# Weaving all attention projections of a mixing layer with the inverse of its blocks, on one Trainium2 core

## The chip, the cores and the metric

The kernel runs as one program on one core of a Trainium2 chip. The metric is the device time of one execution in microseconds (us). A profiled execution adds a trace of every engine: PE is TensorE's matmuls, PEld its weight loads, DVE is VectorE, ACT is ScalarE, POOL is GpSimd, SP is the engine that issues most DMAs.

## The reference

The reference is a network of two blocks on 512 positions of width 1024 in float32. The first (gated MLP, chunked attention, two feed-forward parts) is not touched. The second has a mixing layer and a mixture of 64 experts. The mixing layer is what the change is about: one input projection feeds eight heads of an attention with forget gates ("fox") and eight heads of a linear recurrence ("rwkv7"), and both are joined by an output projection.

```
h = rms_norm(x, norm1_g) * (1 + sc1) + sh1
z = h @ w_in
y_fox  = fox_mixer(z[..., :FOX_COLS], ...)     # q, k, v, g of 512 columns each, gates
y_rwkv = rwkv7_mixer(z[..., FOX_COLS:], ...)   # r, k, v of 512 columns each, low-rank gates
x = x + g1 * (concatenate([y_fox, y_rwkv]) @ w_out)

fox:   k = a_k * shift_prev(k) + (1 - a_k) * k         # v the same way, with a_v
       q = rms_norm(q, qn_g); k = rms_norm(k, kn_g)
       p = softmax(q k^T * scale + (cum_i - cum_j), causal)
       o = rms_norm(p v, on_g) * sigmoid(g)
rwkv7: Sa = S a_t
       S  = S * w_t + Sa b_t + v_t k_t                 # one 64x64 state per head, 512 steps
       y_t = S r_t
```

## The kernel before, in words

The mixing layer works on transposed data, features on the partitions and the 512 positions along the free axis. Heads go in pairs: a pair is 128 features. There are four pairs of rwkv and four of fox.

**Projections.** `zdense` (L880) makes 128 columns of a projection. `wpiece` (L888) loads the 512 KB weight piece (`zraw`, on SP's queue), ScalarE rounds it to `zhi`, and the engine in `self.zlo` subtracts to get the low part `zlo` (L899). `zmm` (L902) then adds three products for each of eight slices of the inner dimension (L907, L908, L909: high by high, high by low, low by high), 24 matmuls of 512 columns. The buffers `zraw`, `zhi` and `zlo` are double.

**The rwkv side.** The recurrence is done in four time chunks of 128. `rwkv_pair` (L950) makes the operands of one pair: the two gate products (`lw` L963, `la` L967), the projection of k, a normalization (the head sum `hs<-sq`), the scaled operands `at` and `bt`, two copies of `bt` padded with zeros on GpSimd (`BP`, L1008), the Gram products `pg` (L1013), their masked copy `g` on DVE (L1015) which goes to DRAM in `gab`, then the projections of r and v, and a closing head sum (`hs<-rk`, L869 by way of L1028). `solve` (L1034) loads the blocks of all Gram matrices as `XL` and inverts 32-row triangular blocks by forward substitution: for each of 31 columns a product (`soltmp<-XL`, L1051 or L1055) and a reduction (L1052 or L1056), all on DVE and each needing the one before; then a copy (L1057), the way out to DRAM and back. After that `rwkv_front` and `rwkv_back` work through 16 blocks (4 chunks by 4 pairs); the first instruction of a block on TensorE is the product `mg<-xx,gz` at L1104.

**The fox side.** `fox_z` (L1263) makes for pair m the four projections k, q, v, g. k and v are mixed with their shifted copies in `shift_mix`: three GpSimd operations on `d` (L1279 to L1281) and a DVE addition (L1282). `fox_qkv` (L1296) normalizes k and q (head sum on TensorE, a chain on DVE and ScalarE) and transposes v. `fox_att` (L1327) is the softmax attention of one pair: scores `pS`, transposed probabilities `pT`, products `pO`.

**What sets the order.** The program is written in one order, and a scheduler reorders each engine's instructions by a simulated timeline. `mixing` (L1472) issues the four rwkv pairs, then `fox_z(0)`, `fox_qkv(0)` and `fox_z(1)`; then the inverse; then everything else through `weave` (L1382). There each stream is a generator that yields an estimate of its TensorE time and of a pause, and the stream with the earliest due time is issued next, in the order of the letters of `WEAVE`. The streams: `rwkv_fronts` (which begins by waiting `SOLVE` = 34 us of simulated time), `rwkv_backs`, `fox_rest` (the attentions, begins after `ATT` = 28 us), `fox_qkvs`, `fox_zs`, `rwkv_outs` and `mix_begin` (the first pieces of the output projection). In the weave `self.zlo` is GpSimd, before it DVE. `tc.issue_after(x)` adds an edge to the scheduler's order on an instruction's own engine: what is issued inside stands behind x in that engine's queue; instructions of other engines are not held by it.

```
for m in range(4):
    self.rwkv_pair(m, R)
for m in range(2):
    for _ in self.fox_z(m):
        pass
    if m == 0:
        for _ in self.fox_qkv(m):
            pass
```

After the layer, the experts' buffers take over the memory of the mixing layer.

Of the kernel before, what the change touches and what calls it, by code (L numbers as in the profile page):

```python
# [11 lines left out]
AF = mybir.ActivationFunctionType  # L12
# [25 lines left out]
class Builder:  # L38
# [260 lines left out]
    def col(self, n, k):  # L299
        r, _ = self.cols[n]  # L300
        return self.colt[:, r + k:r + k + 1]
# [648 lines left out]
    def rwkv_pair(self, m, R):  # L950

        self.mark(f"rwkv_pair{m}")
        nc = self.nc
        sl = slice(m * 128, m * 128 + 128)
        col = lambda n: self.col(n, m)
        T = lambda n, b=1: R.tile([128, S], F32, name=n, tag=n, bufs=b)
        c4 = lambda t: t.rearrange("p (c t) -> p c t", c=NT)

        def out(i, t):
            nc.sync.dma_start(self.fd[m, :, :, i, :].rearrange("c f t -> f c t"), c4(t))  # L960

        ps = self.ps.tile([128, S], F32, name="lw", tag="rk", bufs=2)
        nc.tensor.matmul(ps, self.dup[:, sl], self.twd, start=True, stop=True)  # L963
        s = T("s", 2)
        nc.scalar.activation(s, ps, AF.Sigmoid, bias=col("rw_w0_2"))
        ps = self.ps.tile([128, S], F32, name="la", tag="rk", bufs=2)
        nc.tensor.matmul(ps, self.dup[:, sl], self.tad, start=True, stop=True)  # L967
        ah = T("ah", 2)
        nc.scalar.activation(ah, ps, AF.Sigmoid, bias=col("rw_a0_2"))
        cs = T("cs", 2)  # L970
        nc.vector.tensor_tensor_scan(cs, self.scan_mask, s, 0.0, op0=ALU.mult, op1=ALU.add)

        F = self.F[m]
        mid = self.z2.tile([128, NT, 1], F32, name=f"mid{m}")
        nc.vector.tensor_copy(mid, c4(cs)[:, :, 63:64])
        nc.vector.tensor_sub(F, c4(cs)[:, :, 127], mid[:, :, 0])
        nc.vector.tensor_add(F[:, 0:NT - 1], F[:, 0:NT - 1], mid[:, 1:, 0])
        nc.scalar.activation(F, F, AF.Exp, scale=-self.E05)
        nc.vector.tensor_sub(c4(cs), c4(cs), mid.to_broadcast([128, NT, 128]))
        nc.gpsimd.tensor_sub(s, cs, s)  # L980
        Em = T("Em", 2)
        nc.scalar.activation(Em, cs, AF.Exp, scale=self.E05)
        nc.scalar.activation(cs, cs, AF.Exp, scale=-self.E05)
        exp = nc.scalar.activation(s, s, AF.Exp, scale=-self.E05)
        Ep, Ex = cs, s
        if m == 0:
            with self.tc.issue_after(exp.ins):
                self.fox_forget(R)
        k = T("k")
        self.zdense(((self.RW0 + 512 + 128 * m, 128),), lambda ps: self.mixed(4 + m, ps, k))  # L990
        kk, sq = T("kk"), T("sq")
        nc.scalar.activation(kk, k, AF.Copy, scale=col("rw_k_k_2"))
        nc.scalar.activation(sq, kk, AF.Square)
        hs = self.head_sums(sq, "rk")
        xe, y, n1 = T("xe"), T("y"), T("n1")
        nc.vector.tensor_scalar(xe, hs, 1e-24, None, op0=ALU.max)
        self.newton_rsqrt(xe, y, n1, sq)
        nc.vector.tensor_mul(kk, kk, y)
        at, bt, kt, kn = T("at"), T("bt"), T("kt"), T("kn")
        nc.vector.scalar_tensor_tensor(at, kk, -1.0, Ex, op0=ALU.mult, op1=ALU.mult)  # L1000
        out(1, at)
        nc.gpsimd.tensor_mul(kk, kk, ah)
        nc.vector.tensor_mul(bt, kk, Em)
        out(2, bt)

        BP = self.BP
        for j in range(2):
            nc.gpsimd.tensor_copy(BP[j][64 * j:64 * j + 64], bt[64 * j:64 * j + 64])  # L1008
        for c in range(NT):
            cc = slice(c * 128, c * 128 + 128)  # L1010
            pg = self.ps.tile([128, 2, 128], F32, name="pg", tag="rk", bufs=2)
            for j in range(2):
                nc.tensor.matmul(pg[:, j], BP[j][:, cc], at[:, cc], start=True, stop=True)  # L1013
            g = R.tile([128, 2, 128], F32, name="g", tag="g", bufs=2)
            nc.vector.tensor_mul(g, pg, self.mS[:, None, :].to_broadcast([128, 2, 128]))  # L1015
            nc.sync.dma_start(self.gab[:, c, 2 * m:2 * m + 2, :], g)
        nc.scalar.activation(kn, ah, AF.Identity, scale=col("rw_k_a_2"), bias=self.cols2[:, 16 + m:17 + m])
        nc.vector.tensor_mul(kn, kn, k)
        nc.vector.tensor_mul(kt, kn, Em)
        out(3, kt)  # L1020
        r, rt, rk, v = T("r"), T("rt"), T("rk"), T("v")
        self.zdense(((self.RW0 + 128 * m, 128),), lambda ps: self.mixed(m, ps, r))
        nc.vector.tensor_mul(rt, r, Ep)
        out(0, rt)
        nc.vector.scalar_tensor_tensor(rk, r, col("rw_r_k_2"), kn, op0=ALU.mult, op1=ALU.mult)
        self.zdense(((self.RW0 + 1024 + 128 * m, 128),), lambda ps: self.mixed(8 + m, ps, v))
        out(4, v)
        hs = self.head_sums(rk, "rk")  # L1028
        last = nc.vector.tensor_mul(rk, hs, v)
        nc.sync.dma_start(self.svd[m], rk)  # L1030
        with self.tc.issue_after(last.ins):
            self.x1(2 * m)
# [230 lines left out]
    def fox_z(self, m):  # L1263

        self.mark(f"fox_z{m}")
        nc = self.nc
        scr = self.foxscr
        T = lambda n, b=1: self.fox.tile([128, S], F32, name=n, tag=n, bufs=b)
        mix = []
        for i in range(2):  # L1270
            t = T(f"mixb{i}")
            for j in range(2):
                nc.sync.dma_start(t[64 * j:64 * j + 64], scr[8 + 8 * i + 2 * m + j:9 + 8 * i + 2 * m + j].to_broadcast([64, S]))
            mix.append(t)

        def shift_mix(z, g, ps):
            d = T("d")
            nc.scalar.copy(z, ps)
            nc.gpsimd.tensor_sub(d[:, 1:], z[:, :S - 1], z[:, 1:])  # L1279
            nc.gpsimd.tensor_scalar(d[:, 0:1], z[:, 0:1], -1.0, None, op0=ALU.mult)  # L1280
            nc.gpsimd.tensor_mul(d, d, g)  # L1281
            nc.vector.tensor_add(z, z, d)  # L1282

        zk, zq, zv = T("zk", 2), T("zq", 2), T("zv", 2)
        sg = self.sgm[m] = T("sgm", 4)
        self.zdense(((512 + 128 * m, 128),), lambda ps: shift_mix(zk, mix[0], ps))
        yield 5.2, 0.9
        self.zdense(((128 * m, 128),), lambda ps: nc.scalar.copy(zq, ps))
        yield 5.2, 0.9
        self.zdense(((1024 + 128 * m, 128),), lambda ps: shift_mix(zv, mix[1], ps))  # L1290
        yield 5.2, 0.9
        self.zdense(((1536 + 128 * m, 128),), lambda ps: nc.scalar.activation(sg, ps, AF.Sigmoid))
        yield 5.2, 0.9
        self.zs[m] = zk, zq, zv

    def fox_qkv(self, m):  # L1296
# [110 lines left out]
    def rwkv_fronts(self, W, W2):  # L1407
        yield 0.0, self.SOLVE
        for c in range(NT):
# [11 lines left out]
    def fox_rest(self, W):  # L1421
        yield 0.0, self.ATT
        for m in range(4):
# [2 lines left out]
            self.nfox = m + 1  # L1426

    def fox_zs(self):
        for m in range(2, 4):
            yield from self.fox_z(m)  # L1430

    def fox_qkvs(self):
        for m in range(1, 4):
            yield lambda: m in self.zs and self.nfox > m - 2
            yield from self.fox_qkv(m)

# [29 lines left out]

    KORDER = (0, 1, 2, 4, 5, 3, 6, 7)
    WEAVE = "abfqzmo"
    SOLVE = 34.0
    ATT = 28.0  # L1470

    def mixing(self):  # L1472
        tc, nc, a = self.tc, self.nc, self.a
# [17 lines left out]
        with self.pool(name="rp", bufs=1) as R:  # L1491
            self.BP = [R.tile([128, S], F32, name=f"BP{j}") for j in range(2)]
            for j in range(2):
                nc.gpsimd.memset(self.BP[j][64 * (1 - j):64 * (1 - j) + 64], 0.0)
            with self.tc.issue_after(self.last_x.ins):
                self.x1_rstd(R)
            self.rwkv_lora(R)
            self.fps.close()
            self.mmtags = (("mm", 2),)
            self.zps = ExitStack()  # L1500
            self.ps = self.zps.enter_context(self.pool(name="zps", bufs=1, space=PSUM))
            for m in range(4):
                self.rwkv_pair(m, R)
            for m in range(2):
                for _ in self.fox_z(m):
                    pass
                if m == 0:
                    for _ in self.fox_qkv(m):
                        pass
        self.zps.close()  # L1510
        self.mmtags, self.zlo = (("fs", 2),), nc.gpsimd
        self.ps = self.zps.enter_context(self.pool(name="zps2", bufs=1, space=PSUM))
        with self.pool(name="ck", bufs=1) as W:
            with self.pool(name="sol", bufs=1) as sol:
# [992 lines left out]
```

## Time and profile before

| | |
|---|---|
| three runs | 2319.68, 2321.45, 2327.68 us (median 2321.45) |
| profiled execution, own time | 2325.68 us |
| its span in the trace | 2323.6 us |
| mean granted clock of TensorE, share of full | 0.978 |
| TensorE matmul busy | 2194.9 us, 94% of the span |
| VectorE busy | 1385.3 us, 60% |
| ScalarE busy | 1020.4 us, 44% |
| GpSimd busy | 425.0 us, 18% |

The span is the time from the first to the last instruction in the trace, 2.1 us less than the execution's own time. The shares are means over the whole program. The mixing layer takes the stretch from about 1160 us to 1640 us, where the page's row of TensorE in 40 slices has its two lowest inner digits (8 and 6) and the row of the granted clock its only 8 and 6. All times below are microseconds from the start of the span.

### The profile page before, as it was taken

The page shows a single profiled execution, that of the slowest core. Times are in us where ns is not written, and L with a number is a line of the kernel's source. Part 1 is how long each engine was busy: PE and PEld are TensorE (multiplying, and loading weights), DVE is VectorE, ACT ScalarE, POOL GpSimd, SP SyncE. Part 2 cuts the span into 40 slices and gives each one's busy share as a digit, 9 for nine tenths or more (in the row PEclk, how much of TensorE's full clock was granted, in tenths as well). Part 3 has the DMA queues.
Part 4 walks back from the last instruction along what each step waited for, and adds up shares of the span by engine and source line. Part 5 has one row for each costly group of instructions (what it writes and reads, how often), then busy time and mean ns, then how long its engine had stood idle before and what let it go on. Part 6 is the DMA issues. An engine that isn't in the chain of part 4 may idle for free. (4 is left out here: it accounts for less than half of the span.)

```text
span 2323.6 us, 31933 instructions
## 1 busy us (share of the span) xinstructions
PE 2194.9 (94%) x11699; PEld 1669.0 (72%) x11699; DVE 1385.3 (60%) x2479; ACT 1020.4 (44%) x1759; POOL 425.0 (18%) x354
## 2 busy tenths in 40 slices
PE   8999999999999999999889969999999999999995
PEld 6888888888777888888766657776666757554662
DVE  3658837854887686477557693775444837421343
ACT  4336525534886454345455524652423526211231
POOL 3023203310000322122302440002112111111110
PEclk9999999999999999999999986999999999999998
DMA  4335535435221434344045533226379999999895
GB/s 159 100 119 188 161 96 181 146 100 143 64 64 55 154 118 145 127 135 152 31 119 145 136 92 91 76 71 208 144 268 384 343 327 390 327 333 375 277 388 206
DMA packets 243810, 414.78 MB, mean 179 GB/s; under 512 B 35077, under 2 KB 135779, under 8 KB 243653
## 3 DMA queue, kind: packets, MB, share of 16 engines
q1 hardware_dynamic: 233444, 393.87, 48.8%
q0 software_dynamic: 5184, 13.71, 3.2%
q10 hardware_dynamic: 5024, 5.15, 0.9%
q8 instruction: 93, 1.52, 0.3%
q14 instruction: 65, 0.52, 0.1%
HBM read 378.93 MB, written 40.22 MB: 180 GB/s over the span
## 5 line engine op out<-in xcount | busy, mean ns | idle before, releaser
L93 DVE TENSOR_TENSOR wlo<-wraw,whi 128x2048 fp32r<-128x2048 f32 (+3 forms) x83 | 182.6, 2200 | 208.3 <-ACT whi L92 207.9
L135 PE MATMUL mm<-sgh,whi 128*128 128x512 f32 x768 | 300.8, 392 | 0.9 <-DVE hT L204 0.9
L136 PE MATMUL mm<-sgl,whi 128*128 128x512 f32 x768 | 299.3, 390 | 0.0
L137 PE MATMUL mm<-sgh,wlo 128*128 128x512 f32 x768 | 297.6, 389 | 0.0
L92 ACT CAST whi<-wraw 128x2048 fp32r<-128x2048 f32 (+3 forms) x83 | 146.2, 1761 | 211.2 <-PE mm L136 158.9
L746 POOL TENSOR_TENSOR adaacc<-adaacc,adaw 128x512 f32<-128x512 f32 x84 | 147.6, 1757 | 433.9 <-ACT adaw L745 430.7
L2181 POOL DMA_INDIRECT racc<-y,idx x60 | 88.8, 1479 | 470.3 <-DVE y L2171 401.3
L135 PEld LDWEIGHTS mm<-sgh,whi 128*128 128x128 f32 x768 | 144.2, 188 | 30.9 <-issue 1.5
L137 PEld LDWEIGHTS mm<-sgh,wlo 128*128 128x128 f32 x768 | 144.2, 188 | 30.4 <-issue 0.2
L136 PEld LDWEIGHTS mm<-sgl,whi 128*128 128x128 f32 x768 | 144.2, 188 | 29.8 <-issue 0.5
L2125 PE MATMUL pg<-er,xh 128*64 128x512 f32 (+1 forms) x768 | 152.2, 607 | 9.6 <-DMA er<-in_exp_w_up 9.6
L2054 ACT CAST eh<-er 128x512 fp32r<-128x512 f32 x200 | 116.3, 620 | 80.0 <-DMA er<-in_exp_w_up 42.7
L135 PE MATMUL mm<-ach,whi 128*128 128x512 f32 (+1 forms) x374 | 141.4, 378 | 0.0
L137 PE MATMUL mm<-ach,wlo 128*128 128x512 f32 (+1 forms) x374 | 140.9, 377 | 0.0
L136 PE MATMUL mm<-acl,whi 128*128 128x512 f32 (+1 forms) x374 | 140.8, 377 | 0.0
L2058 DVE TENSOR_TENSOR el<-er,eh 128x512 fp32r<-128x512 f32 x200 | 125.9, 685 | 13.6 <-ACT eh L2054 13.2
L2125 PEld LDWEIGHTS pg<-er,xh 128*64 128x64 f32 (+1 forms) x768 | 46.3, 130 | 105.8 <-issue 103.7
L907 PE MATMUL mm<-nmh,zhi 128*128 128x512 f32 (+2 forms) x264 | 106.3, 404 | 10.5 <-DVE k L877 5.8
L2136 ACT ACTIVATE sg<-pg 128x256 f32<-128x256 f32 x40 | 15.4, 384 | 214.8 <-PE pg L2125 214.5
L908 PE MATMUL mm<-nml,zhi 128*128 128x512 f32 (+2 forms) x264 | 103.7, 393 | 1.4 <-DVE nml L809 1.4
L909 PE MATMUL mm<-nmh,zlo 128*128 128x512 f32 (+2 forms) x264 | 102.9, 390 | 1.8 <-DVE zlo L899 1.8
L2171 DVE TENSOR_TENSOR y<-py,g2b 128x512 f32<-128x512 f32 x76 | 52.3, 690 | 87.6 <-PE py L2168 87.6
(702 smaller groups left out, 5187.2 us busy)
## 6 DMA issues: line engine op xcount, KB each, us to landing
er<-in_exp_w_gate SPq DMA_DIRECT2D x128, 512.0 KB
er<-in_exp_w_up SPq DMA_DIRECT2D x128, 512.0 KB
er<-in_exp_w_down SPq DMA_DIRECT2D x64, 1024.0 KB
wraw<-in_f_w_in SPq DMA_DIRECT2D x32, 1024.0 KB
adaw<-in_ada_w SPq DMA_DIRECT2D x96, 256.0 KB
wraw<-in_f_w_down SPq DMA_DIRECT2D x16, 1024.0 KB
zraw<-in_w_in SPq DMA_DIRECT2D x30, 512.0 KB
wraw<-in_a_w_in SPq DMA_DIRECT2D x8, 1024.0 KB
```

Of the source, the lines that this page charges most:

```text
L92: nc.scalar.copy(hi[:, :n], raw[:, :n])
L93: nc.vector.tensor_sub(lo[:, :n], raw[:, :n], hi[:, :n])
L135: nc.tensor.matmul(to, wh[:, cols], xh, start=first, stop=False)
L136: nc.tensor.matmul(to, wh[:, cols], xl, start=False, stop=False)
L137: nc.tensor.matmul(to, wl[:, cols], xh, start=False, stop=last)
L746: nc.gpsimd.tensor_add(acc, acc, t)
L907: nc.tensor.matmul(ps[:n, part], hi[:, k, :n], xh, start=first and k == ks[0], stop=False)
L908: nc.tensor.matmul(ps[:n, part], hi[:, k, :n], xl, start=False, stop=False)
L909: nc.tensor.matmul(ps[:n, part], lo[:, k, :n], xh, start=False, stop=last and k == ks[-1])
L2054: nc.scalar.copy(hi, r)
L2058: nc.vector.tensor_sub(lo, r, hi)
L2125: nc.tensor.matmul(job["pg"][b:b + n], x[:, c:c + n], job["raw"][j][h][:, k % 4] if whole else job["gu"][j][k][w], start=k == 0 and i == 0 ...
```

## The change

All sixteen fox projections are issued in the weave, none before the inverse. Each of them is put behind the last Gram product on TensorE by `issue_after(self.last_gram.ins)`. In the weave the low parts are made on VectorE. The weave's simulated waits are 52 instead of 34 us for the blocks and 45 instead of 28 us for the attentions.

```diff
@@ rwkv_pair
-                nc.tensor.matmul(pg[:, j], BP[j][:, cc], at[:, cc], start=True, stop=True)
+                self.last_gram = nc.tensor.matmul(pg[:, j], BP[j][:, cc], at[:, cc], start=True, stop=True)
@@ fox_z
-        self.zdense(((512 + 128 * m, 128),), lambda ps: shift_mix(zk, mix[0], ps))
-        yield 5.2, 0.9
-        self.zdense(((128 * m, 128),), lambda ps: nc.scalar.copy(zq, ps))
-        yield 5.2, 0.9
...
+        for c, evac in ((512, lambda ps: shift_mix(zk, mix[0], ps)), (0, lambda ps: nc.scalar.copy(zq, ps)),
+                        (1024, lambda ps: shift_mix(zv, mix[1], ps)),
+                        (1536, lambda ps: nc.scalar.activation(sg, ps, AF.Sigmoid))):
+
+            with self.tc.issue_after(self.last_gram.ins):
+                self.zdense(((c + 128 * m, 128),), evac)
+            yield 5.2, 0.9
@@ fox_zs, fox_qkvs
-        for m in range(2, 4):
+        for m in range(4):
             yield from self.fox_z(m)
...
-        for m in range(1, 4):
+        for m in range(4):
             yield lambda: m in self.zs and self.nfox > m - 2
@@ weave
-    SOLVE = 34.0
-    ATT = 28.0
+    SOLVE = 52.0
+    ATT = 45.0
@@ mixing
-            for m in range(2):
-                for _ in self.fox_z(m):
-                    pass
-                if m == 0:
-                    for _ in self.fox_qkv(m):
-                        pass
         self.zps.close()
-        self.mmtags, self.zlo = (("fs", 2),), nc.gpsimd
+        self.mmtags, self.zlo = (("fs", 2),), nc.vector
```

The scheduler's answer to this is seen in the order of the instructions on an engine. The first place is TensorE between the closing head sum of pair 2 (`hs<-rk`) and the Gram products of pair 3. Before, the queue begins there with:

```order
L869 MATMUL hs<-rk,blk 128x512
L907 MATMUL mm<-nmh,zhi 128x512
L908 MATMUL mm<-nml,zhi 128x512
L909 MATMUL mm<-nmh,zlo 128x512
L869 MATMUL hs<-sq,blk 128x512
L963 MATMUL lw<-twd,dup 128x512
L967 MATMUL la<-tad,dup 128x512
L907 MATMUL mm<-nmh,zhi 128x512
```

The last of these rows is the start of further projection matmuls, which go on until pair 3's Gram products. Now the same place is, on TensorE, from pair 2's closing head sum to pair 3's:

```order
L869 MATMUL hs<-rk,blk 128x512
L963 MATMUL lw<-twd,dup 128x512
L967 MATMUL la<-tad,dup 128x512
L869 MATMUL hs<-sq,blk 128x512
L1013 MATMUL pg<-at,BP_9343 128x128 x2
L1013 MATMUL pg<-at,BP_9344 128x128 x2
L1013 MATMUL pg<-at,BP_9343 128x128
L1013 MATMUL pg<-at,BP_9344 128x128
L1013 MATMUL pg<-at,BP_9343 128x128
L1013 MATMUL pg<-at,BP_9344 128x128
L869 MATMUL hs<-rk,blk 128x512
L907 MATMUL mm<-nmh,zhi 128x512
```

The projections of k, r and v of pair 3 stand ahead of pair 2's Gram products now, and no projection stands between the two pairs' Gram products. The first fox projection is the last row. Between pair 1's and pair 2's Gram products 48 projection matmuls are left of 72. Behind the last Gram product, nine projections (216 matmuls) stand ahead of the first block product; the other seven stand among the rows of the blocks.

The second place is VectorE inside the inverse (`soltmp` and `XL` are its steps, `zlo` a projection's low part, `zk<-zk,d` the addition of the shifted mix). Before:

```order
L1051 TENSOR_TENSOR soltmp<-XL 128x128
L1052 TENSOR_REDUCE XL<-soltmp 128x2x8
L1051 TENSOR_TENSOR soltmp<-XL 128x162
L1052 TENSOR_REDUCE XL<-soltmp 128x2x9
L1051 TENSOR_TENSOR soltmp<-XL 128x200
L1052 TENSOR_REDUCE XL<-soltmp 128x2x10
L1051 TENSOR_TENSOR soltmp<-XL 128x242
L1052 TENSOR_REDUCE XL<-soltmp 128x2x11
L1051 TENSOR_TENSOR soltmp<-XL 128x288
```

In this piece the steps follow each other without anything between them. Now the same steps on VectorE are:

```order
L1051 TENSOR_TENSOR soltmp<-XL 128x128
L1052 TENSOR_REDUCE XL<-soltmp 128x2x8
L1282 TENSOR_TENSOR zk<-zk,d 128x512
L1051 TENSOR_TENSOR soltmp<-XL 128x162
L1052 TENSOR_REDUCE XL<-soltmp 128x2x9
L1051 TENSOR_TENSOR soltmp<-XL 128x200
L1052 TENSOR_REDUCE XL<-soltmp 128x2x10
L1051 TENSOR_TENSOR soltmp<-XL 128x242
L899 TENSOR_TENSOR zlo<-zraw,zhi 128x1024
L1052 TENSOR_REDUCE XL<-soltmp 128x2x11
L1051 TENSOR_TENSOR soltmp<-XL 128x288
L1052 TENSOR_REDUCE XL<-soltmp 128x2x12
```

A low part and an addition of the mix stand between steps; over the whole inverse eight low parts and four such additions do.

The third place is TensorE in the second block, from its product `mg<-xx,gz` at L1134 on (`pT`, `pO` and `pS` are the attention's). Now:

```order
L1134 MATMUL mg<-xx,gz_10292 64x64 x2
L1340 MATMUL pS<-ka_9327,qa_9325 128x384
L1156 MATMUL pr<-tm,gg 128x64
L1110 MATMUL pt<-ident,ft 128x128 x3
L1357 MATMUL pO<-vn,PT 128x64
L1352 MATMUL pT<-ident,P 128x128 x2
L907 MATMUL mm<-nmh,zhi 128x512
L908 MATMUL mm<-nml,zhi 128x512
L909 MATMUL mm<-nmh,zlo 128x512
```

The last three rows are the start of the first of the seven projections that stand among the blocks; before, no fox projection is left behind the first block product. (Lines of the changed kernel behind L1292 are one lower than before.)

## Rows read from the trace of the kernel before

**Rows 1.** Busy time by stretch: us, PE, PEld, DVE, ACT, POOL, PEclk, DMA share, GB/s.

```profile
1170.40:1252.30 81.90, 71.22 (x294) 53.78 (x294) 50.28 (x72) 44.75 (x59) 8.76 (x8) 0.96 0.47 132
1252.30:1318.10 65.80, 61.96 (x272) 47.92 (x271) 46.76 (x67) 40.24 (x52) 22.50 (x18) 1.00 0.44 123
1318.10:1408.00 89.90, 65.92 (x274) 50.11 (x273) 68.10 (x102) 28.00 (x44) 41.26 (x39) 0.85 0.47 114
1408.00:1439.00 31.00, 30.11 (x195) 24.71 (x196) 10.80 (x37) 10.65 (x27) 0.00 (x0) 0.50 0.28 80
1439.00:1600.40 161.40, 152.82 (x1310) 117.73 (x1309) 115.60 (x333) 83.31 (x213) 9.51 (x25) 1.00 0.27 81
```

**Rows 2.** Timeline of TensorE at the milestones: start, us, instruction, [idle before, releaser].

```profile
1243.52 1.05 PE L1013 MATMUL pg<-at,BP 128*128 128x128 f32 x8
...
1247.15 1.13 PE L869 MATMUL hs<-rk,blk 128*128 128x512 f32 x2 [1.13 <-DVE g L1015]
...
1269.08 1.05 PE L1013 MATMUL pg<-at,BP 128*128 128x128 f32 x8
...
1322.11 1.02 PE L869 MATMUL hs<-rk,blk 128*128 128x512 f32 x2
...
1407.97 0.43 PE L1104 MATMUL mg<-xx,gz 128*32 128x32 f32 x8 [1.39 <-DMA xx<-xdr]
```

**Rows 3.** Longest wait of TensorE, 1318 to 1408 us: total, times, longest.

```profile
PE pT L1353 <- ACT P L1345: 14.8, 1, 14.8
```

**Rows 4.** Timeline of GpSimd: the padded copies of pair 2.

```profile
1264.95 2.14 POOL L1008 COPY BP<-bt 64x512 f32<-64x512 f32 x2 [0.86 <-DVE bt L1003]
```

**Rows 5.** Timeline of VectorE: a low part and an operation of 512 columns.

```profile
1199.27 1.22 DVE L899 TENSOR_TENSOR zlo<-zraw,zhi 128x1024 fp32r<-128x1024 f32 x1
...
1335.46 0.69 DVE L1309 TENSOR_SCALAR xe<-hs 128x512 f32<-128x512 f32 x1
```

**Rows 6.** Timeline from the masked copies to the first step of the inverse.

```profile
1246.67 0.88 DVE L1015 TENSOR_TENSOR g<-pg,mS 128x256 f32<-128x256 f32 x2 [0.40 <-DMA gab<-g]
...
1320.09 0.76 DVE L1015 TENSOR_TENSOR g<-pg,mS 128x256 f32<-128x256 f32 x2 [5.16 <-DMA gab<-g]
...
1326.21 5.07 SPq L1043 DMA_DIRECT2D XL<-gab  x4
...
1335.07 0.36 DVE L1051 TENSOR_TENSOR soltmp<-XL 128x2 f32<-128x2 f32 x1 [3.24 <-DMA XL<-gab]
```

**Rows 7.** VectorE busy during the inverse: its products and reductions through soltmp; everything.

```profile
1335.00:1393.00 58.00, 44.03 (x62) 0.84 0.33 93
...
1335.00:1393.00 58.00, 55.41 (x82) 0.84 0.33 93
```

**Rows 8.** Timeline inside the inverse: two operations of GpSimd, four of VectorE.

```profile
1346.79 2.39 POOL L899 TENSOR_TENSOR zlo<-zraw,zhi 128x1024 fp32r<-128x1024 f32 x1 [5.08 <-ACT zhi L898]
1351.11 1.30 POOL L1281 TENSOR_TENSOR d<-d,mixb 128x512 f32<-128x512 f32 x1
...
1346.95 2.63 DVE L1051 TENSOR_TENSOR soltmp<-XL 128x200 f32<-128x200 f32 x1
...
1350.01 0.94 DVE L1051 TENSOR_TENSOR soltmp<-XL 128x242 f32<-128x242 f32 x1
...
1351.43 1.54 DVE L1051 TENSOR_TENSOR soltmp<-XL 128x288 f32<-128x288 f32 x1
...
1389.74 2.80 DVE L1057 COPY XL<-XL 128x1024 f32<-128x1024 f32 x1
```

**Rows 9.** Timeline of TensorE: first and last of 72 projection matmuls.

```profile
1340.09 0.47 PE L907 MATMUL mm<-nmh,zhi 128*128 128x512 f32 x1
...
1356.29 0.40 PE L909 MATMUL mm<-nmh,zlo 128*128 128x512 f32 x1
```

**Rows 10.** Timeline of TensorE: a projection after an idle stretch, eleven matmuls apart.

```profile
1189.04 0.79 PE L907 MATMUL mm<-nmh,zhi 128*128 128x512 f32 x1 [5.77 <-DVE k L877]
...
1193.41 0.40 PE L908 MATMUL mm<-nml,zhi 128*128 128x512 f32 x1
```

## What the change does to the time, predicted

> **What bounds the kernel now.** I read the engine busy times by stage first [rows 1]. From the first pair of the mixing layer to the first weight piece of its output projection (1170 to 1600 us) TensorE is busy 382 of 430 us, so most of what it does there is on the path, and what can be won is the idle part and the part at half clock. The reader should see where these are: the pairs up to 1252 (10.7 us idle), the stretch between the last Gram product and the first block (24.0 us idle, granted clock 0.85) and the first 31 us of the blocks (granted clock 0.50, which is 1.2 GHz). Next comes the timeline of TensorE at the milestones: Gram products of pair 1 and 2, the head sum that closes the last pair (1322.11), the first block product (1407.97) [rows 2]. The last Gram product starts a serial chain that no matmul can shorten: its masked copy goes to DRAM, comes back as XL, DVE inverts 32-row blocks in 62 small steps, the result goes to DRAM and back. In the list of waits of TensorE for that stretch the longest is one of 14.8 us on a softmax that stands behind the inverse on DVE [rows 3]. After 1640 us come the experts; their buffers reuse the mixing layer's memory, so I pass a shift of 1600 us through to the end one to one.
>
> **The change, part by part.** I follow four milestones, in this profiled execution (span 2323.6, own time 2325.68; the median of the runs is 2321.45, so 4.2 us under it).
>
> 1. *The last Gram comes earlier.* In the new order TensorE has no projection between pair 2's Gram products and pair 3's (order pieces in the section on the change); seven of the eight moved projections, and one set of normalizations, leave the stretch before the last Gram. Until 1252 nothing differs. Then TensorE has 48 matmuls instead of 72 and is through at about 1263.7, but pair 2's Gram products need both padded copies of POOL, ready at 1264.95 + 2.14 = 1267.1 [rows 4], against 1269.08 now [rows 2]. From there pair 3 is a latency chain on DVE, ACT and POOL. Its length is seen one pair earlier, where no attention work stood in it: pair 1's Gram starts at 1243.52, pair 2's could start at 1267.1, 23.6 us. The new chain has no projection low part in it (1.22 on DVE [rows 5]) and no next pair's k (0.7, estimated from the other 512-column DVE operations [rows 5]), so 21.7: pair 3's Gram at 1288.8. Pair 1 then took 3.6 us to its closing head sum (1243.52 to 1247.15): 1292.4, against 1322.11. **-29.7 us.** Bounds: -31 if the first Gram products go as soon as the first padded copy is there; -27 if the chain keeps its 23.6 and half clock adds to the Grams. I take the middle, since the dropped operations are on DVE's queue, which the chain uses. The price is that TensorE now idles some 20 us in pair 3.
>
> 2. *Gram to inverse.* Now 13.0 us pass from the head sum to the first step of the inverse (1335.07), among them a masked copy that waits 5.16 us for the DMA of the one before, and an XL load issued at 1326.21 behind two weight pieces and two gate rows on SP's queue [rows 6]. In the new order none of these stands there; pair 1's copy waited 0.4 us [rows 6]. With 1.9 us for the last masked copy's DMA and the 8.9 us from the XL issue to the first step I get 1303.7, 11.3 us. **-1.7 us** (bounds 0 and -3).
>
> 3. *The inverse itself.* It takes 57.4 us (1335.07 to 1392.5). DVE is busy 55.4 us in the window, 44.0 of them with the steps' 62 instructions [rows 7]. Seven steps are far longer than their neighbours: 2.63 us beside POOL's low part of 2.39 us, while the next but one, larger, takes 0.94 [rows 8]. Interpolating between neighbours the seven are 9.3 us too long, and the final copy some 1.6: about 10.9 us lost to POOL. Four of POOL's low parts lie inside. With the low parts on DVE those blockings go, but eight low parts now stand between the steps in DVE's order, 1.15 us each once overlap with a dependent step is counted (1.22 alone [rows 5]): +9.2. POOL's shift-mix stays on POOL: three sets lie inside, 1.3 us each by the step that took 1.54 beside one, where 0.68 would fit [rows 8]: +3.9. Pair 0's two normalizations now lie inside whole, one did before, less softmax work: +0.8. So -10.9 + 9.2 + 3.9 + 0.8 = **+3.0 us**. Bounds: -5 if the sets of POOL cost nothing, +8 if each blocks for its whole 2.6 us and a low part waits for its cast.
>
> The Trainium skill (SBUF — State Buffer, "Who interferes with whom") says that DVE and GpSimd share a port pair as an exclusive lock: a two-input DVE operation and a GpSimd operation that reads SBUF exclude each other, and the later one waits in full. The 2.63 us step agrees with that. By its rule the three remaining sets could cost up to their whole length, and the term would be +6.6 instead of +3.0, the sum 3.6 us worse; I keep the row's price, since most sets fall partly on operations with one input.
>
> 4. *Inverse to first block.* 15.5 us of transfers (1392.5 to 1407.97), unchanged: **0**. TensorE's rows ahead of the first block product are nine projections and four softmax steps, all ready before: it waits for xx as now. First block at 1407.97 - 29.7 - 1.7 + 3.0 = 1379.6.
>
> 5. *The blocks.* Before, all sixteen projections were done at the first block. In the new order nine are; seven are spread over blocks 2 to 12. One projection is 24 matmuls; 72 of them start from 1340.09 to 1356.29 [rows 9], 0.228 apart, so 5.47 us each, **+38.3 us**. One normalization, one set of transposes and two softmax steps more are left: **+2.0**. Can the blocks hide them? From 1439 to 1600 TensorE is busy 152.8 of 161.4 us [rows 1], so there are 8.6 us of holes, partly in the tail. Half clock costs 15 us of the 31 [rows 1]. The first woven projection stands behind two blocks, which at 1.2 GHz take some 24 us; after an idle stretch a projection is back at full clock after some ten matmuls, as the two rows from 1189.04 on show (0.79 us, then 0.40) [rows 10]. So the slow stretch shrinks by a few us: I take **-3** for clock and holes together. Bounds: 0 (the fillers wait for their low parts as often as they fill), and -23.6 (all holes and all of the clock's cost).
>
> Sum: -29.7 - 1.7 + 3.0 + 38.3 + 2.0 - 3.0 = **+8.9 us**. On the median: 2330.4, so I say **2330 us**. In one sentence: the Gram comes 30 us earlier, by moving 38 us of TensorE's work from a stretch where it was nearly free, since the pair chain left holes for it, to the blocks, where TensorE has none.
>
> **The rivals.**
>
> *Faster: the clock and the holes pay for the weave.* The place is the first 30 us of blocks. If TensorE comes out of the inverse at 2.4 GHz, because dense projections stand right before the first block, the 15 us are won, and the 8.6 us of holes are filled too. Then the sum is +8.9 + 3.0 - 23.6 = -11.7, 2310 us. It decides when the granted clock of the first two blocks is 1.0. For it: nine projections fill the wait. Against it: DVE hands out their low parts over the whole inverse, so they come apart by more than their length and the last softmax steps leave TensorE idle, as the 14.8 us wait does now. Chance 0.17.
>
> *No net effect: the inverse gets shorter.* If POOL's rest costs nothing and the pair chain starts 1 us sooner, the sum is +8.9 - 8 - 1 = 0, 2321 us. For it: the 10.9 us lost now are large. Against: DVE's queue is full there. Chance 0.12.
>
> *Much slower: DVE's queue couples the inverse to TensorE.* Low parts wait for weight pieces, casts and freed buffers; DVE works in order, so each such wait delays the steps behind it. With +8 in place of +3 on the inverse, no relief in clock or holes, and 5 more in the tail, where the last attention now ends beside the last blocks: +21.9, 2343 us. Chance 0.13. That the change does not do what it says is ruled out by the order.
>
> **How the numbers follow.** The forecast has 0.58, with its own range 2322 to 2340. A measurement of this kernel tells 0.3%, 7 us, from no change, so the limits are 2314.5 and 2328.4. Forecast: 0.37 of its 0.58 lies above 2328.4, 0.21 inside. Slower rival: 0.13 slower. Faster rival: 0.14 faster, 0.03 same. No net effect: 0.03 faster, 0.08 same, 0.01 slower. Slower 0.51, same 0.32, faster 0.17. The range 2310 to 2345 leaves out about half of the faster rival and half of the slower one, some 0.17.
>
> **What would show it.** In the new profile: last Gram near 1291, with TensorE mostly idle from 1272 to 1288 and a granted clock at 0.5 there; first inverse step near 1304; 60 us to its copy; first block near 1380; the output projection's first piece, now at the end of the last window of [rows 1], 9 us later. Steps of 2.4 us or more should be gone from the inverse, and DVE should show eight low parts in it. I am wrong in step 1 if the Gram is not before 1300, in step 3 if the inverse takes under 54 or over 66 us, in step 5 if blocks 1 to 16 and the tail take under 215 us, where I expect 229.

## The result and the profile after

The changed kernel takes 2346.93 us (median of four runs, 2339.15 to 2347.98) against 2321.43 us before (median of four runs, one more than above); the ratio is 1.0099, with a 95% interval from 1.0077 to 1.0121. It is slower by one per cent. The profiled execution took 2346.36 us with a span of 2344.6 us, 21.0 us over the span before. The medians are 25.5 us apart, since the profiled execution of the kernel before was 4 us slower than its median. The page's first lines, against 2194.9, 1385.3 and 1020.4 us before:

```profile
span 2344.6 us, 31944 instructions
...
PE 2203.4 (94%) x11699; PEld 1675.2 (71%) x11699; DVE 1384.5 (59%) x2489; ACT 1015.5 (43%) x1754; POOL 399.8 (17%) x344
...
PEclk9999999999999999999998889989999999999998
```

The milestones first: TensorE's timeline, the rows that answer to [rows 2], and the two ends of the inverse on VectorE.

```profile
1266.78 1.38 PE L1013 MATMUL pg<-at,BP 128*128 128x128 f32 x8 [2.66 <-POOL BP L1008]
...
1288.92 4.08 PE L1013 MATMUL pg<-at,BP 128*128 128x128 f32 x16 [11.12 <-POOL BP L1008]
...
1293.40 1.13 PE L869 MATMUL hs<-rk,blk 128*128 128x512 f32 x2 [0.40 <-DVE g L1015]
...
1376.76 0.43 PE L1104 MATMUL mg<-xx,gz 128*32 128x32 f32 x8 [0.23 <-DMA xx<-xdr]
...
1613.93 0.50 PE L907 MATMUL mm<-ysh,zhi 128*128 128x512 f32 x1 [0.35 <-ACT zhi L898]
```

```profile
1301.62 0.86 DVE L1051 TENSOR_TENSOR soltmp<-XL 128x2 f32<-128x2 f32 x1 [5.04 <-DMA XL<-gab]
...
1360.18 1.08 DVE L1057 COPY XL<-XL 128x1024 f32<-128x1024 f32 x1
```

Pair 3's Gram products start at 1288.92. The closing head sum comes 28.7 us earlier than before, the first block 31.2 us earlier, and yet the last row, which answers to the end of the windows of [rows 1], comes 13.4 us later. (The prediction calls it the output projection's first piece. It is the third of eight: the first two stand among the blocks, and the output projection's first product starts at 1562.74 us before and at 1588.94 us now.) The same stretches as in [rows 1], cut at the new milestones (columns as there):

```profile
1170.40:1252.30 81.90, 71.22 (x295) 53.87 (x294) 49.95 (x72) 44.66 (x59) 8.76 (x8) 0.96 0.45 131
1252.30:1290.00 37.70, 22.27 (x79) 14.81 (x79) 27.34 (x44) 19.96 (x27) 8.69 (x8) 0.76 0.39 118
1290.00:1376.80 86.80, 69.26 (x282) 53.02 (x283) 68.18 (x112) 29.07 (x44) 20.09 (x29) 0.87 0.47 114
1376.80:1407.80 31.00, 28.92 (x204) 23.31 (x205) 16.60 (x41) 15.28 (x36) 0.00 (x0) 0.82 0.23 64
1407.80:1613.80 206.00, 193.73 (x1486) 151.95 (x1484) 127.58 (x352) 92.59 (x225) 18.58 (x34) 0.94 0.28 85
```

Read these rows as a balance of TensorE. Its work is the same in both kernels, so the length of the mixing layer is that work, plus the time in which TensorE idles, plus what half clock costs. I worked the last one out from windows of 2.5 us: busy time times what the granted clock lacks to 1. From 1170 us to the first transposes behind the layer (`ph<-ident,hT`):

| | length | idle | cost of half clock | work at full clock |
|---|---|---|---|---|
| before | 473.9 | 48.3 | 22.9 | 402.7 |
| changed | 491.9 | 60.8 | 28.2 | 402.9 |

Each row is one execution, and half clock differs between executions of one kernel: the mean granted clock of the kernel before went from 0.974 to 0.982 in its runs. The 18.0 us are 12.5 of idle time and 5.3 of half clock. By stretch (idle and half clock together): the pairs up to the closing head sum 16.6 before, 33.5 now; from there to the first block 29.6 and 22.5; the blocks 21.3 and 26.4; the tail 3.6 and 6.4. So the idle time went up where the projections were taken out, and it was not won back where they were put. The other 3 us lie in the experts, whose length from that point to the end is 682.7 us against 679.7, in a scatter of 679 to 686 over all profiles of this study.

### The profile page after: what moved, and what is told of

Its sections match the earlier page's. It is cut to its first block, busy times and chain, and to the rows that moved or that the text cites. A ratio compares the mean times of both kernels' runs of the same rounds, so it can differ in the third digit from the quotient of the medians.

```text
span 2344.6 us, 31944 instructions
## 1 busy us (share of the span) xinstructions
PE 2203.4 (94%) x11699; PEld 1675.2 (71%) x11699; DVE 1384.5 (59%) x2489; ACT 1015.5 (43%) x1754; POOL 399.8 (17%) x344
## 5 line engine op out<-in xcount | busy, mean ns | idle before, releaser
L137 PEld LDWEIGHTS mm<-sgh,wlo 128*128 128x128 f32 x768 | 144.1, 188 | 30.2 <-issue 0.2
```

The lines of the kernel that those rows point to most:

```text
L137: nc.tensor.matmul(to, wl[:, cols], xh, start=False, stop=last)
```

## The experiments

All theories in the expectations refer to this balance: A says that TensorE's moved work decides, B blames VectorE's low parts, C the due times, and the rivals are named where they stand. Each ratio is to runs of the kernel before that were taken with the experiment. Their medians lie between 2320.3 and 2323.9 us, so a difference between the absolute times of two experiments is good to about 3 us.

**1. Low parts back on GpSimd.**

```diff
-        self.mmtags, self.zlo = (("fs", 2),), nc.vector
+        self.mmtags, self.zlo = (("fs", 2),), nc.gpsimd
```

> The changed kernel with one edit undone: the low parts of the woven projections go back to GpSimd. Theory A (TensorE's moved work): VectorE was not what made the change slow; in the inverse the eight low parts leave VectorE's queue (8 x 1.2 us) but each blocks a step for some 2.7 us, so the inverse grows from 59.7 to about 70 us, the first block goes from 1376.8 to about 1387, and the time is 2350 to 2358. Theory B (VectorE's low parts couple the inverse and the blocks to TensorE): the inverse falls under 57 us and the blocks run closer together, 2325 to 2335.

Measured 2364.31 us, ratio to before 1.0199 (1.0168 to 1.0230). VectorE's low parts are not what makes the changed kernel slow: with them on GpSimd it is 17 us slower still. This run alone says only that GpSimd is the worse place; that VectorE's low parts cost nothing against the kernel before is what experiments 3 and 7 show. The inverse took 64.6 us, not 70. The busy time of its 62 steps, first with low parts on VectorE, then on GpSimd:

```profile
1301.60:1361.30 59.70, 38.09 (x62) 0.88 0.38 106
```

```profile
1303.50:1368.10 64.60, 46.37 (x62) 0.85 0.35 93
```

The same 62 steps took 8.3 us longer beside GpSimd's eight low parts, one us for each and not the 2.7 that I took. The time beyond my 2358 was lost in the blocks, which took 239.3 us to their last gate product against 228.9, half of the difference by half clock (17.6 against 12.3 us).

**2. The due times as before** (52 and 45 back to 34 and 28 in the changed kernel).

> The changed kernel with the two simulated waits of the weave as before, 34 and 28 us instead of 52 and 45: seven projections instead of nine stand ahead of the first block, nine among the blocks, and the last attention ends three blocks earlier. Theory A (TensorE's moved work): the first block is set by the inverse, so two more projections cost 2 x 5.5 us in the blocks, of which the gap of TensorE beside the last attention (9 us of idle time from 1527 to 1560) gives something back: 2345 to 2358. Theory C (the new due times put the work badly): 2325 to 2335.

Measured 2354.68 us, 1.0153 (1.0126 to 1.0181): 8 us slower than the changed kernel, within A. The first block came at 1375.2; with nine projections instead of seven the blocks hold more of TensorE's work (214 against 202 us at full clock).

**3. The low parts alone, in the kernel before** (the line of the first experiment the other way round).

> The kernel before with one part of the change alone: the low parts in the weave on VectorE instead of GpSimd; the projections stay where they were. Theory A with the prices of my prediction: the inverse, 57.5 us before, loses the four blockings (-10.9 us) and gains four low parts (+4.6 us), so it takes about 51 us and the kernel 2312 to 2318. Theory B (low parts in VectorE's queue delay the steps behind them): 2322 to 2332.

Measured 2324.08 us, 1.0016 (1.0001 to 1.0031). Both expectations had the mechanism wrong. The blockings did go, as A said (VectorE's busy time in the inverse: the steps, then the low parts):

```profile
1330.20:1390.30 60.10, 37.01 (x62) 0.86 0.38 109
...
1330.20:1390.30 60.10, 9.17 (x7) 0.86 0.38 109
```

The steps fell from 44.0 us [rows 7] to 37.0, and the final copy from 2.8 us to 1.1. But a low part costs VectorE about what the blocking did: seven low parts take 9.2 us of it. GpSimd had six in the inverse before, not the four that the expectation counts. With five more softmax operations and one more addition of the mix inside, and 1.1 us more of idle time, the inverse takes 60.1 us instead of 57.5. The time stays within 0.3% of the kernel before. The profiled execution was the fastest of the ten, 7 us under the median, so its blocks (7.8 us shorter than before, most of that by the clock) don't show what this zero is made of.

**4. Pair 0 stays ahead of the inverse.**

```diff
             for m in range(4):
                 self.rwkv_pair(m, R)
+            for _ in self.fox_z(0):
+                pass
+            for _ in self.fox_qkv(0):
+                pass
...
     def fox_zs(self):
-        for m in range(4):
+        for m in range(1, 4):
```

> The changed kernel with the four projections and the normalizations of fox pair 0 issued ahead of the inverse as before, and without the edge for these four; pairs 1 to 3 stay woven. 96 of TensorE's projection matmuls go back into the holes of rwkv pairs 2 and 3, ten projections stand ahead of the first block, two of the sixteen are left in the blocks. Theory A (holes in the pairs are nearly free, the blocks are not): the last Gram comes some 10 us later than in the changed kernel (about 1299 instead of 1289), five projections leave the blocks (-27 us) and the gap beside the last attention closes: 2315 to 2328. Rival D (the first Gram product early is what counts, and the blocks wait for VectorE and ScalarE rather than for TensorE): the 10 us are lost and the blocks give back less than 10, 2340 to 2350.

Measured 2325.68 us, 1.0020 (1.0007 to 1.0033): 21 us of the loss are gone with four projections. TensorE in the pairs up to the closing head sum, and in the blocks up to the last gate product:

```profile
1170.00:1312.90 142.90, 117.36 (x489) 89.39 (x487) 93.47 (x137) 79.94 (x103) 25.73 (x22) 0.92 0.45 127
...
1396.80:1588.20 191.40, 183.63 (x1555) 143.24 (x1555) 128.77 (x371) 98.89 (x249) 7.79 (x22) 0.98 0.26 76
```

The time came out as A said, but not by A's reason. Pair 3's Gram products start at 1308.2, 19 us later than in the changed kernel instead of 10, and the closing head sum 19.5 us later, for 96 matmuls that are 21.9 us at 0.228 us each. So the holes in the pairs were not nearly free for these four projections: idle time and half clock of the pairs fell only from 33.5 to 30.2 us. The gain is in the blocks, which take 191.4 instead of 228.9 us. Of these 37.5 us, 23 are TensorE's work (five projections less, twelve matmuls of the output projection and a few others more) and 15 are idle time and half clock (26.4 in the changed kernel, 11.6 here, 21.3 before).

**5. The projections ahead of the normalizations.**

```diff
-    WEAVE = "abfqzmo"
+    WEAVE = "abfzqmo"
```

> The changed kernel with one edit: in the weave's list of streams the projections stand ahead of the normalizations, so ten instead of nine projections stand ahead of the first block, the last one stands in block 8 instead of block 12, and the last attention ends as early as in the kernel before. Low parts, due times and Gram products are as in the changed kernel. Theory A with the gap (late projections leave the last attention without cover: TensorE idle 8 us more in the blocks than before, and half clock behind them): one projection less in the blocks (-5.5 us), the gap and the half clock after it gone (-8 to -11), one low part more in the inverse (+1.2): 2329 to 2340. Rival (the idle time only turns up in another place): 2341 to 2350.

Measured 2334.39 us, 1.0054 (1.0039 to 1.0069), 12.5 us less than the changed kernel, as A with the gap had it. (In the trace the last projection stands in block 5, from 1453.1 us on, and not in block 8.) What the gap is, is seen in the changed kernel, where the last projection's last product starts at 1523.57. Its window, and TensorE's timeline in it:

```profile
1515.00:1560.00 45.00, 35.38 (x229) 26.64 (x229) 31.84 (x76) 21.18 (x47) 2.21 (x3) 0.77 0.21 61
```

```profile
1540.89 1.91 PE L869 MATMUL hs<-sq,blk 128*128 128x512 f32 x2
...
1542.60 1.06 PE L1321 MATMUL pv<-ident,zv 128*128 128x128 f32 x4
...
1547.51 0.80 PE L1176 MATMUL py<-ft,P 128*128 128x128 f32 x2 [3.85 <-DVE xe L1209]
...
1549.29 1.22 PE L1340 MATMUL pS<-ka,qa 66*128 66x128 f32 x4
```

On VectorE at the same time:

```profile
1543.18 0.69 DVE L1308 TENSOR_SCALAR xe<-hs 128x512 f32<-128x512 f32 x1
...
1546.90 0.55 DVE L1209 TENSOR_SCALAR xe<-hs 128x384 f32<-128x384 f32 x1
```

Attention 3 needs the normalizations of pair 3 (`hs<-sq` at 1540.89 is the second of them), and these are issued only when all four projections of the pair are, so no projection is left to run beside them. The longest wait, 3.85 us, is that of a product of the blocks for an operation of VectorE (L1209) that stands behind this normalization (L1308 and the three operations after it) in VectorE's queue. In all TensorE idles 9.6 of these 45 us, and the granted clock is 0.77 in them.

The whole blocks, up to the last gate product, of the kernel before, of the changed kernel and of this one:

```profile
1408.00:1593.30 185.30, 179.09 (x1488) 139.96 (x1488) 121.84 (x358) 91.83 (x235) 4.91 (x19) 0.92 0.25 73
```

```profile
1376.80:1605.70 228.90, 214.77 (x1661) 169.31 (x1661) 139.86 (x378) 105.99 (x255) 12.54 (x26) 0.93 0.26 76
```

```profile
1377.20:1590.40 213.20, 206.58 (x1644) 161.58 (x1643) 138.73 (x382) 108.74 (x261) 13.64 (x26) 0.97 0.28 80
```

Against the changed kernel the idle time falls from 14.1 to 6.6 us, and half clock from 12.3 to 6.2; the one projection less counts for 2.2 us of work.

**6. Seven of eight slices left out of pair 3's projections.**

```diff
-                self.zdense(((c + 128 * m, 128),), evac)
+                self.zdense(((c + 128 * m, 128),), evac, ks=1 if m == 3 else KD)
```

> The changed kernel with seven of eight slices left out of the four projections of fox pair 3 (84 of TensorE's matmuls, all among the blocks; their weights, casts, low parts and everything behind them stay). Leaves out part of the computation. 84 x 0.228 us = 19.2 us. Theory A (TensorE is the bound in the blocks): 17 to 28 us faster than the changed kernel (2346.9), 2319 to 2330. Rival (the blocks wait for VectorE and ScalarE, TensorE's work is covered): less than 8 us faster, 2339 to 2347.

Measured 2319.24 us, 0.9981 (0.9967 to 0.9995): 27.7 us less than the changed kernel for an estimated 19.2 us of matmuls. TensorE bounds the blocks; they take 202.3 instead of 228.9 us:

```profile
1377.90:1580.20 202.30, 193.19 (x1579) 151.07 (x1578) 138.98 (x376) 105.64 (x255) 12.26 (x26) 0.95 0.30 86
```

In the profiled execution, which was 5 us slower than the median, the mixing layer is 25.5 us shorter than in the changed kernel: 17 us of work, and the rest idle time and half clock, which fell with it (60.8 to 55.9 and 28.2 to 24.5 us).

**7. Everything but the move** (the kernel before, with low parts on VectorE and due times 52 and 45).

> The kernel before with the other two parts of the change: low parts in the weave on VectorE, due times 52 and 45; the eight projections of pairs 0 and 1 stay ahead of the inverse. Theory A (the loss is in the moved projections): within 0.3% of the kernel before, 2314 to 2327. Theory C (the due times make it slow): over 2332.

Measured 2322.74 us, 0.9997 (0.9979 to 1.0014). The other two parts of the change do nothing by themselves; the loss comes with the moved projections. The move without the other two parts was not run; with only one of them taken back (experiments 1 and 2) it was slower.

**8. Pair 0 ahead of the inverse, due times 60 and 60.**

> The fourth experiment's kernel (pair 0 ahead of the inverse) with due times 60 and 60 instead of 52 and 45: eleven projections instead of ten stand ahead of the first block, one is left in the blocks. Theory A: one projection less in the blocks (-5.5 us) against one low part more in the inverse (+1.2) and an attention that begins later (0 to +6): 2319 to 2328. Rival (TensorE stays idle in the inverse while the attention waits): 2329 to 2340.

Measured 2320.61 us, 0.9994 (0.9976 to 1.0011): no different from before, with eleven projections ahead of the first block and one behind. The stretches of its trace, cut as above:

```profile
1170.40:1252.30 81.90, 71.19 (x297) 53.82 (x296) 51.26 (x73) 45.11 (x60) 8.77 (x8) 0.96 0.47 133
1252.30:1308.70 56.40, 41.92 (x180) 32.31 (x178) 40.89 (x61) 34.18 (x43) 16.95 (x14) 0.87 0.42 122
1308.70:1397.00 88.30, 74.71 (x319) 59.24 (x320) 67.64 (x106) 26.31 (x38) 21.89 (x30) 0.93 0.49 118
1397.00:1428.00 31.00, 29.42 (x242) 23.62 (x242) 14.82 (x42) 15.10 (x37) 1.88 (x3) 0.89 0.39 112
1428.00:1590.00 162.00, 154.72 (x1308) 118.55 (x1307) 116.31 (x338) 90.29 (x218) 9.62 (x25) 0.99 0.26 78
```

Here the first 31 us of blocks have a granted clock of 0.89, against 0.50 before, so the faster rival's gain at this place is had. What it hangs on was not tested: in the second experiment, with seven projections ahead of the first block and more idle time there, it was 0.93. But 14.5 us are idle between 1252 and 1309, against 3.8 in the stretch to the last Gram before [rows 1]. Idle time and half clock together, against the kernel before: 13.1 us more in the pairs, 13.1 less from there to the first block, 11.1 less in the blocks, 3.0 more in the tail. These two executions differ by 4.7 us, the medians by none that is clear of noise.

**9 to 11. Less work for VectorE in the inverse.** In `normed` the scaled sum, the square of the root and the gains go to ScalarE:

```diff
-            nc.vector.tensor_scalar(xe, hs, 1.0 / 64, 1e-6, op0=ALU.mult, op1=ALU.add)
-            self.newton_rsqrt(xe, y, n1, sq)
+            nc.scalar.activation(xe, hs, AF.Identity, scale=1.0 / 64, bias=self.eps6)
+            nc.scalar.activation(y, xe, AF.Abs_reciprocal_sqrt)
+            nc.scalar.activation(n1, y, AF.Square)
+            nc.vector.scalar_tensor_tensor(sq, n1, -0.5, xe, op0=ALU.mult, op1=ALU.mult)
+            nc.vector.scalar_tensor_tensor(y, sq, 1.5, y, op0=ALU.add, op1=ALU.mult)
+            nc.vector.tensor_mul(y, y, z)
...
-                nc.vector.scalar_tensor_tensor(dst[0:64, j, :], z[r], gcol[r], y[r], op0=ALU.mult, op1=ALU.mult)
+                nc.scalar.activation(dst[0:64, j, :], y[r], AF.Copy, scale=gcol[r])
```

> The eighth experiment's kernel with the attention's normalization of k and q rewritten: the scaled head sum, the square of the root and the two gains go from VectorE to ScalarE, which is busy 20 of 60 us during the inverse; VectorE keeps three operations of 512 columns instead of six (some 2.2 us less for each normalization, four of them in the inverse). If the inverse is as long as VectorE's work in it (58 of 60 us busy in the changed kernel), it falls from 59.8 to about 52 us and the first block from 1397 to about 1389, and the time to 2310 to 2317. Rival: TensorE, which then has less time for the same projections in the inverse, becomes the bound of that stretch, and the time stays within 2317 to 2326.

> The same rewriting in the seventh experiment's kernel (both early pairs ahead of the inverse, low parts on VectorE, due times 52 and 45). The inverse is 59.6 us there, with two of the normalizations inside at most once the first ones are done early: it falls to about 54 us and the time to 2313 to 2320. Rival: no change beyond 0.3%, 2317 to 2329.

> The same rewriting in the fifth experiment's kernel (all sixteen projections in the weave, projections ahead of the normalizations). If VectorE is what holds the inverse, it falls from 59.1 to about 51 us and the time from 2334 to 2323 to 2329. Rival (TensorE's moved work bounds the blocks, and a shorter inverse gives it less cover): 2330 to 2337.

Measured 2329.63 us (1.0030, 1.0013 to 1.0047), 2326.20 us (1.0019, 1.0005 to 1.0033) and 2334.99 us (1.0052, 1.0021 to 1.0083). The inverse did become shorter, by some 5.5 us in all three (59.8 to 54.1, 59.6 to 54.5, 59.1 to 53.6). No time was won by it: the second stayed within its rival's range, the third too, and the first is beyond both of its ranges, 9 us slower than the eighth experiment. The blocks up to the last gate product, of the eighth and of the ninth:

```profile
1397.00:1583.40 186.40, 179.44 (x1534) 139.26 (x1533) 127.06 (x370) 104.48 (x252) 7.68 (x23) 0.98 0.27 77
```

```profile
1390.10:1593.40 203.30, 193.26 (x1570) 150.31 (x1570) 123.35 (x367) 118.69 (x279) 8.81 (x23) 0.95 0.26 74
```

The first block comes 6.9 us earlier and the blocks last 16.9 us longer: 7 us of TensorE's work were pushed over the border, half clock costs 7 us more, idle time 3. ScalarE, on which the softmax depends, is busy 14 us more there. That its longer chains are the reason for the idle time is likely, not shown.

## Why the prediction was right, and where it was not

The direction was right, and so was the reason that led to it: TensorE's work was moved from a stretch with room for it to one without. The size was not: +21.0 us between the two spans against +8.9 in the sum, and the median of 2346.93 is 1.9 us beyond the range's end (by the ratio it would be 2344). Ahead of the first block the sum was 2.8 us too high; behind it, it was 15 us too low, 8 of them for clock and holes in the blocks. Term by term, from the traces:

- **The last Gram comes earlier:** -28.7 us at the closing head sum, -29.7 forecast, and 1288.92 for pair 3's Gram products against 1288.8. From pair 2's to pair 3's it took 22.1 us, 21.7 forecast from the 23.6 of one pair earlier. The Gram products ran at half clock (4.08 us for sixteen), so the head sum followed after 4.5 us, not 3.6. TensorE idled 12.8 us between the two, where I had said some 20.
- **Gram to inverse:** 13.0 us became 8.2, so -4.8 instead of -1.7. From XL's first issue (1295.91) to the first step it took 5.7 us, not the 8.9 that I took from the row of before. No weight piece stands ahead of it in SP's queue now; that this is the reason was not tried.
- **The inverse:** 59.6 us from the first step to the end of the copy, against 57.5, so +2.2 (+3.0 forecast). Steps of 2.4 us are gone; eight low parts take 10.5 us of VectorE, 9.2 priced. (Six of GpSimd's low parts lay inside before, not four; the sum does not use this count.) Four of GpSimd's sets lie inside, not three. The operations beside them are longer by some 0.3 to 0.8 us each, about 5 us in all by an estimate from their neighbours, against 3.9 priced. One example: a product of 392 elements took 1.63 us at 1315.57, beside a GpSimd operation from 1315.16 to 1316.45; the same product took 0.90 in the fourth experiment. The Trainium skill (SBUF — State Buffer, "Who interferes with whom") says that whoever issues first holds the shared port pair for its whole instruction and the other blocks. The trace agrees: what is left of the GpSimd operation, 0.88 us, is about what the step lost, 0.73. The 2.63 us step of [rows 8] began 0.16 us behind its low part and lost about 2.1 us by its neighbours, nearly the whole.
- **Inverse to first block:** 15.5 us as before; first block at 1376.76, 1379.6 forecast.
- **The blocks:** the work fits the forecast. At full clock it is 202.5 us against 164.0, 38.5 more: 39.0 for the seven projections and 2.5 for the rest (+38.3 and +2.0 forecast), less 3.0 for twelve matmuls of the output projection that stand behind the last gate product now. **The step that failed is the one behind it**, "-3 for clock and holes together". It came out at +5.1. Half clock fell by 2.8 us, as taken. The holes did not shrink; they grew from 6.2 to 14.1 us, because the last projections stand beside blocks 10 to 12 and attention 3 then has nothing beside it. I had seen in the order that the last attention ends beside the last blocks, and gave it 5 us only in the slower rival. The fifth experiment took the gap away and 12.5 us with it.
- **"I pass a shift of 1600 us through to the end one to one"** failed as well: +13.4 us at the output projection's third piece became +18.0 at the transposes behind it. From the last gate product to those transposes it takes 56.2 us, before 50.6. Of the difference, 3.4 us are half clock (around 1608 and 1632; before there was none) and the rest is the twelve matmuls that have come over from the blocks. Idle time is no more than before. All versions with sixteen woven projections take 56.2 to 57.4 us there, with 24 of the 48 matmuls of the output projection's first two pieces ahead of the last gate product; the others take 50.6 to 53.4, with 36 ahead. Why the clock falls there was not tried. The last 3 us are within the experts' scatter.

Of the rivals, the much slower one named 2343 us, near what came, but for the wrong reason: VectorE did not couple the inverse to TensorE, which the third and the seventh experiment show. Its "no relief in clock or holes" and "5 more in the tail" are the parts of it that happened. The faster rival's condition was a granted clock of 1.0 in the first two blocks; it was 0.82 in the first 31 us. Nor is the condition enough: in the eleventh experiment, which has all sixteen projections woven, the granted clock was 1.00 in the first 31 us of the blocks, and that execution took 2331.76 us, not 2310.

What the prediction lacked is a view of the whole balance. I priced the Gram's 30 us as won and 38 as lost, each from its own rows. The balance says it at once: the pairs up to the closing head sum lost 16.9 us of TensorE's time to idling and half clock, the inverse gave back 7.1, and the blocks had only 6.2 us of idle time to give. What more could be had in the blocks was in the clock: in the fourth and the eighth experiment half clock cost 3.9 and 3.3 us there instead of 15.1, with no less idle time than before.

That the Gram products come first is the work of the order in which the program issues the projections. Without the edge on the last Gram product the scheduler puts out the same program, instruction for instruction, so the edge neither costs nor wins anything here.

No version that does the whole computation beat the kernel before. The eighth experiment equals it.

## What to carry to other kernels

Where one engine's work is the same in both versions and it is busy nine tenths of a stretch, add up its idle time and what its lower clock costs, stretch by stretch, before costing any chain: a milestone that comes 30 us earlier is worth only what it takes out of that sum. Work that fills the holes of a latency chain should leave it only for holes elsewhere that are shown in the trace. Ask it of each piece by itself: putting pair 0's four projections back delayed the chain by 19.5 us for 21.9 us of matmuls, while pair 1's four, which the kernel before has there too, add only another 9.3 us to it. When work is spread late, look for the consumer that stands behind its last piece, since that one will have no cover.

## What the runs showed that was not expected

A shorter chain on VectorE did not shorten the kernel. In the last three experiments the inverse lost 5 us, the first block came 4 to 7 us earlier, and the time did not fall in any. And the low parts were little cheaper on VectorE: six on GpSimd had cost the steps and the copy 8.7 us, and seven on VectorE take 9.2 (third experiment). Only in the changed kernel, with eight of them, is the inverse 5 us shorter with the low parts on VectorE (first experiment).
